# Two transformer blocks on one core: the tile scheduler orders the instructions by its timeline simulation

## The chip, the cores and the metric

The kernel runs on one core of one Trainium2 chip. The metric is the device time of one execution in microseconds (us), from a set of runs of which the median is given. Lower is better.

## The reference

The input is one sequence of 256 rows of width 2048. It goes through two blocks of different kinds, all in fp32. Cut to what matters here:

```python
# block 1
mod = silu(c) @ ada_w + ada_b            # (2048) @ (2048, 6*2048): shift, scale, gate, twice
h = rmsnorm(x, norm_mix_g) * (1 + scale_m) + shift_m
p = h @ w_in                             # 2048 x 11344: q, k, v, g, gate rank, latents, two merge gates
y_gla = gla(p) @ gla_wo                  # gated linear attention, 4 heads
y_mla = mla(p) @ mla_wo                  # latent attention, 16 heads, causal, with rope
x = x + gate_m * ((sigmoid(p_ga) * y_gla + sigmoid(p_gb) * y_mla) @ w_out)
h = rmsnorm(x, norm_ffn_g) * (1 + scale_f) + shift_f
x = rmsnorm(x + gate_f * swiglu(h, ffn_w_in, ffn_w_down), final_norm_g)
# block 2, for l in (0, 1)
h = rms_norm(x, pre_norm_g[l])
mixed = concat(retention(h), diff_attention(h), rg_lru(h))
x = x + rms_norm(mixed @ w_out[l], post_norm_g[l])
```

## The kernel before, in words

**The stream of weights.** Each weight matrix is read once, in blocks of 512 KB or 384 KB. `wload` (L172 to L175) gives the load to SP's queue into a tile `raw` (four buffers). `split` (L168 to L170) makes two halves of it for the matmuls: ACT casts the high half (`wh`, L169), DVE subtracts it to get the low half (`wl`, L170); there are six buffers of each. The activations are held split in the same way, as `hh` and `hl` (or `oh` and `ol` for what comes out of an attention).

**The products.** `lin` (L228 to L258) takes the blocks in groups of four and issues, for each 128 rows of weight and each of the two row tiles, three matmuls into one tile `pm` of PSUM (four buffers):

```python
pe.matmul(o, AH[:, k0 + k, sl], L[:, k, 0:nw], ...)   # L247: needs wl and hh
pe.matmul(o, AH[:, k0 + k, sl], H[:, k, 0:nw], ...)   # L248: needs wh and hh
pe.matmul(o, AL[:, k0 + k, sl], H[:, k, 0:nw], ...)   # L249: needs wh and hl
```

**The start stage.** The first projection runs in four groups of 512 rows of the 2048 (the loop over `KG`, from L577 on). In each group the product goes through three column parts: the latents (`latb`), then the two merge gates (`X` and `ga`), then a piece of v. L598 copies the first group's sums out, L600 on DVE adds those of the later groups. A group can start when its part of `mod` is known: the sum `acc` of `ada_w` over its rows (L351, L353 on DVE, from `raw` tiles of its own), four transposes on PE (L314, `tp<-ident,acc`), four row sums on ACT (L316, `adac`), an addition on DVE (L317, `mod<-adac,vc`). Then ACT makes the group's activations (L590, four of them, `ht`), ACT casts them (L169, `hh`) and DVE subtracts (L170, `hl`). The first group's scale does the sum with matmuls on PE instead (L349, `px`); the rows of x are normed and transposed for all groups at the start (L569, L570). The steps of the next group's `ada_w` sum are called between the column parts of the running group.

**The table of angles.** `later()` (L407 to L492) loads gains and positions with small DMAs and works out sines and cosines on DVE (`ext`, `latb`, L439 to L491) and ACT (L488, L492). The program calls it in the last group, after its second column part (`LATER = (3, 1)`).

**The GLA heads.** For each head `gla_att` folds six levels of a decay matrix: DVE and ACT make `gqk`, PE multiplies it with itself (L871, `px<-gqk`), DVE masks the result (L877, `ms`). Between these stand the matmuls of the projection of another part.

**The layer boundary of block 2.** At the end of the first layer DVE adds the normed product to X (L1359, `X<-y,r_y,X`), PE transposes X (L261), ACT and DVE split it into the next layer's `hh` and `hl` (L269, L270).

**What sets the order.** The kernel is written with the tile framework: the program issues instructions in the order of the Python code, and when the context closes, a scheduler puts them into one order for each engine, with the dependencies between them and a priority that counts up as the code is run. An engine runs its own list strictly in that order. The kernel steers the scheduler at a few places: `tc.high_priority(HP)` (L971, L1349) and `tc.issue_after(...)` (L976, L989, L1356) with the constants `PIN` and `PIN2`, the early or late call of generators (`AHEAD`, `LATER`, `PREP`), and the number of buffers. The context is opened in `kernel`.

## Time and profile before

| | before |
|---|---|
| median of 3 runs | 2666.24 us |
| lowest and highest of them | 2661.85, 2666.38 us |
| the profiled execution: its time, its span | 2668.47 us, 2666.7 us |
| mean granted clock of TensorE | 0.992 |
| busy: PE, DVE, ACT | 2590.0, 1829.1, 1332.0 us |
| read from memory | 555.77 MB |

The span runs from the first to the last instruction of the profiled execution, and its time lies 1.8 us above it. PE is TensorE's matmuls, PEld its weight loads, DVE VectorE, ACT ScalarE, SP the engine that issues the DMAs. A matmul with 512 columns is listed with 0.39 us, and one starts every 0.23 us, since they overlap.

### The profile page before, as it was taken

To read this page: it belongs to the slowest core of one execution; us is meant where nothing else is said; L and a number is where in the kernel's file an instruction comes from. 1 tells how busy PE (TensorE), PEld (TensorE's weight loads), DVE (VectorE), ACT (ScalarE), POOL (GpSimd) and SP (SyncE) were. 2 spreads that over 40 slices of the span, in tenths; PEclk is the share of its full clock that TensorE was granted. 3 is DMA by queue.
4 is the path that set the end of the run, shared out by engine and by line. 5 is a ranking of instruction groups with operands and counts; after the bars stand their busy time and mean duration, and the time that the engine had idled before them with its cause. 6 is when DMAs were issued, how large, how long until landed. Compare 5 with 4: busy or idle time off the path is not lost.

```text
span 2666.7 us, 35520 instructions
## 1 busy us (share of the span) xinstructions
PE 2590.0 (97%) x12980; PEld 2196.0 (82%) x12980; DVE 1829.1 (69%) x3043; ACT 1332.0 (50%) x2068; POOL 0.2 (0%) x4
## 2 busy tenths in 40 slices
PE   7999999999999998999999999999999999999998
PEld 4888888877888776777888888889988988997897
DVE  5899877778777777667554555467676657676755
ACT  4545754345555334443344434455565546465653
POOL 0000000000000000000000000000000000000000
PEclk9999999999999999999999999999999999999999
DMA  9898746586576887788655555565455565655464
GB/s 325 317 308 248 221 135 218 186 268 218 179 237 210 283 281 248 237 267 273 203 190 189 189 190 189 190 195 181 149 170 171 185 201 167 189 171 153 160 205 146
DMA packets 319672, 562.84 MB, mean 211 GB/s; under 512 B 23812, under 2 KB 100488, under 8 KB 319240
## 3 DMA queue, kind: packets, MB, share of 16 engines
q1 hardware_dynamic: 319496, 560.56, 65.2%
q8 instruction: 102, 1.67, 0.3%
q14 instruction: 74, 0.61, 0.1%
HBM read 555.77 MB, written 4.72 MB: 210 GB/s over the span
## 4 chain that ended last, share of the span: by engine, by line
PE 69%; DMA 14%; DVE 9%; ACT 5%; issue 2%; SPq 0%; ACTq 0%; DVEq 0%
PE pm L247 19%; PE pm L248 19%; PE pm L249 19%; DMA raw<-in_ada_w_dram 6%; DVE wl L170 4%; ACT wh L169 3%; DMA raw<-in_w_in_dram 3%; DVE acc L353 2%; DMA raw<-in_w_out_dram 2%; DMA raw<-in_ffn_w_in_dram 2%; DMA raw<-in_gla_wo_dram 1%; DMA raw<-in_mla_wo_dram 1%; PE px L871 1%; PE tp L261 1%; PE pm L637 1%
## 5 line engine op out<-in xcount | busy, mean ns | idle before, releaser
L170 DVE TENSOR_TENSOR wl<-raw,wh 128x1024 fp32r<-128x1024 f32 (+2 forms) x876 | 1005.1, 1155 | 469.7 <-ACT wh L169 444.5
L169 ACT CAST wh<-raw 128x1024 fp32r<-128x1024 f32 (+2 forms) x876 | 871.2, 998 | 817.0 <-PE pm L249 415.7
L247 PE MATMUL pm<-wl,hh 128*128 128x512 f32 (+2 forms) x2448 | 925.6, 378 | 21.7 <-DVE wl L170 15.4
L248 PE MATMUL pm<-wh,hh 128*128 128x512 f32 (+2 forms) x2448 | 913.5, 373 | 0.0
L249 PE MATMUL pm<-wh,hl 128*128 128x512 f32 (+2 forms) x2448 | 912.8, 373 | 0.0
L247 PEld LDWEIGHTS pm<-wl,hh 128*128 128x128 f32 x2448 | 462.1, 189 | 98.3 <-DVE wl L170 27.7
L248 PEld LDWEIGHTS pm<-wh,hh 128*128 128x128 f32 x2448 | 462.6, 189 | 62.9 <-issue 2.7
L249 PEld LDWEIGHTS pm<-wh,hl 128*128 128x128 f32 x2448 | 461.7, 189 | 63.9
L247 PE MATMUL pm<-wl,oh 128*128 128x512 f32 x864 | 342.4, 396 | 3.8 <-DVE wl L170 3.6
L249 PE MATMUL pm<-wh,ol 128*128 128x512 f32 x864 | 337.9, 391 | 0.0
L248 PE MATMUL pm<-wh,oh 128*128 128x512 f32 x864 | 337.6, 391 | 0.0
L353 DVE SCALAR_TENSOR_TENSOR acc<-raw,cT,acc 128x512 f32<-128x512 f32 x345 | 258.0, 748 | 71.4 <-DMA raw<-in_ada_w_dram 66.1
L247 PEld LDWEIGHTS pm<-wl,oh 128*128 128x128 f32 x864 | 162.6, 188 | 40.9 <-DVE wl L170 7.6
L249 PEld LDWEIGHTS pm<-wh,ol 128*128 128x128 f32 x864 | 162.6, 188 | 34.3
L248 PEld LDWEIGHTS pm<-wh,oh 128*128 128x128 f32 x864 | 162.8, 188 | 33.0 <-issue 0.5
L213 PE MATMUL pm<-hh,wl 128*128 128x256 f32 x256 | 74.3, 290 | 3.5 <-DVE wl L170 3.5
L214 PE MATMUL pm<-hh,wh 128*128 128x256 f32 x256 | 73.1, 286 | 0.0
L215 PE MATMUL pm<-hl,wh 128*128 128x256 f32 x256 | 72.9, 285 | 0.0
L213 PEld LDWEIGHTS pm<-hh,wl 128*128 128x128 f32 x256 | 49.7, 194 | 5.3 <-DVE wl L170 3.9
L214 PEld LDWEIGHTS pm<-hh,wh 128*128 128x128 f32 x256 | 49.7, 194 | 0.9 <-issue 0.9
L170 DVE TENSOR_TENSOR ol<-tp,oh 128x512 fp32r<-128x512 f32 (+1 forms) x38 | 23.7, 629 | 38.5 <-ACT oh L169 38.5
L215 PEld LDWEIGHTS pm<-hl,wh 128*128 128x128 f32 x256 | 49.6, 194 | 0.0
(396 smaller groups left out, 2087.0 us busy)
## 6 DMA issues: line engine op xcount, KB each, us to landing
raw<-in_w_in_dram SPq DMA_DIRECT2D x224, 512.0 KB
raw<-in_ada_w_dram SPq DMA_DIRECT2D x192, 512.0 KB
raw<-in_ffn_w_in_dram SPq DMA_DIRECT2D x176, 512.0 KB
raw<-in_w_in_dram SPq DMA_DIRECT2D x192, 384.0 KB
raw<-in_w_out_dram SPq DMA_DIRECT2D x96, 512.0 KB
raw<-in_ffn_w_down_dram SPq DMA_DIRECT2D x88, 512.0 KB
raw<-in_mla_wo_dram SPq DMA_DIRECT2D x32, 512.0 KB
raw<-in_gla_wo_dram SPq DMA_DIRECT2D x32, 512.0 KB
```

What stands on the lines that cost most here:

```text
L169: act.copy(H, src)
L170: vec.tensor_sub(L, src, H.bitcast(F32))
L213: pe.matmul(o, L[:, k, c], AH[:, k0 + k], start=k0 + k == 0, stop=False)
L214: pe.matmul(o, H[:, k, c], AH[:, k0 + k], start=False, stop=False)
L215: pe.matmul(o, H[:, k, c], AL[:, k0 + k], start=False, stop=k0 + k == KA - 1)
L247: pe.matmul(o, AH[:, k0 + k, sl], L[:, k, 0:nw], start=first, stop=False)
L248: pe.matmul(o, AH[:, k0 + k, sl], H[:, k, 0:nw], start=False, stop=False)
L249: pe.matmul(o, AL[:, k0 + k, sl], H[:, k, 0:nw], start=False, stop=last)
L261: pe.transpose(ps[:, q], src[:, q * P:(q + 1) * P], ident)
L353: vec.scalar_tensor_tensor(acc[:, 0:w], r[:, k], col, acc[:, 0:w], ALU.mult, ALU.add)
L637: pe.matmul(ps, L, A[0][:, k], start=k == 0, stop=False)
L871: pe.matmul(o[:, t], qk[:, f, sl], rhs, start=f == 0, stop=f == 1)
```

## The change

One argument is added where the context is opened. The scheduler then chooses the next instruction by a simulation of the engines' timelines instead of by its plain ready times. The code that issues instructions isn't touched.

```diff
@@ -1394,7 +1394,7 @@
         aps[n] = nc.dram_tensor(f"in_{n}_dram", a.shape, mybir.dt.from_np(a.dtype), kind="ExternalInput").ap()
     out = nc.dram_tensor("out_0_dram", (1, S, D), F32, kind="ExternalOutput").ap()
-    with tile.TileContext(nc) as tc:
+    with tile.TileContext(nc, schedule_with_timeline_sim=True) as tc:
         tile_two_blocks(tc, aps, out)
     r = _run(nc, [arrays], core_ids=[0])
     return r.results[0]["out_0_dram"]
```

The set of instructions is the same before and after (12526 matmuls and transposes on PE, 3045 instructions on DVE, 1210 on SP). Their order differs on every engine: on average an instruction stands 11 places from where it stood on PE and on DVE, 5 on ACT and 3 on SP. Three places follow.

**The first loads, on SP.** Before, behind the loads of x:

```order
L174 DMA raw<-in_ada_w_dram 128x2x512 x2
L575 DMA X<-in_x_dram 128x2048 x2
L174 DMA raw<-in_ada_w_dram 128x2x512 x15
L174 DMA raw<-in_w_in_dram 128x2x368 x2
L174 DMA raw<-in_ada_w_dram 128x2x512
```

and now:

```order
L174 DMA raw<-in_ada_w_dram 128x2x512 x2
L575 DMA X<-in_x_dram 128x2048 x2
L174 DMA raw<-in_ada_w_dram 128x2x512 x5
L412 DMA latb<-in_norm_ffn_g_dram 16x128
L414 DMA latb<-in_pre_norm_g_dram 16x128 x2
L174 DMA raw<-in_ada_w_dram 128x2x512 x2
L415 DMA latb<-in_mla_q_norm_g_dram 4x128
L416 DMA latb<-in_mla_kv_norm_g_dram 4x128
L417 DMA latb<-in_diff_subln_g_dram 2x128
L418 DMA latb<-in_gla_onorm_g_dram 4x128
L419 DMA latb<-in_diff_subln_g_dram 2x128
L435 DMA pos_i<-in_positions_dram 128x2x1
```

The small loads of `later()` (thirteen with those that follow) have come from far behind to between the first loads of `ada_w`; three of the `ada_w` loads that stand there now are those of the second group.

**The start of the third group, on PE and DVE.** `tp_1380`, `adac_1381` and `ht_1472` are the third group's transposes, row sums and activations; `pm_1479` is its first product, `pm_1433` the last of the second group; `acc_1519` is already the sum for the fourth group. PE before, at the transposes:

```order
L247 MATMUL pm_1337<-wl_1347,hh_114 128x512
L248 MATMUL pm_1337<-wh_1346,hh_114 128x512
L249 MATMUL pm_1337<-wh_1346,hl_115 128x512
L314 MATMUL tp_1380<-ident_79,acc_1147 128x128 x4
L247 MATMUL pm_1392<-wl_1397,hh_114 128x512
L248 MATMUL pm_1392<-wh_1396,hh_114 128x512
```

and now:

```order
L247 MATMUL pm_1433<-wl_1443,hh_114 128x512
L248 MATMUL pm_1433<-wh_1442,hh_114 128x512
L249 MATMUL pm_1433<-wh_1442,hl_115 128x512
L314 MATMUL tp_1380<-ident_79,acc_1147 128x128 x4
L247 MATMUL pm_1433<-wl_1443,hh_114 128x512
L248 MATMUL pm_1433<-wh_1442,hh_114 128x512
L249 MATMUL pm_1433<-wh_1442,hl_115 128x512
L247 MATMUL pm_1479<-wl_1484,hh_114 128x368
L248 MATMUL pm_1479<-wh_1483,hh_114 128x368
```

Before, 48 matmuls stood between the transposes and the third group's first product; now three do. DVE before, from the end of the second group on:

```order
L170 TENSOR_TENSOR wl_1443<-raw_1440,wh_1442 128x1024
L317 TENSOR_TENSOR mod_100<-adac_1381,vc_95 128x4
L170 TENSOR_TENSOR wl_1484<-raw_1481,wh_1483 128x736
L600 TENSOR_TENSOR ga_124<-pm_1392,ga_124 128x512
L351 TENSOR_SCALAR acc_1519<-raw_1520,cT_98 128x512
L353 SCALAR_TENSOR_TENSOR acc_1519<-raw_1520,cT_98,acc_1519 128x512
L353 SCALAR_TENSOR_TENSOR acc_1519<-raw_1524,cT_98,acc_1519 128x512
L600 TENSOR_TENSOR ga_124<-pm_1393,ga_124 128x512
L170 TENSOR_TENSOR hl_115<-ht_1472,hh_114 128x1024
```

and now, from the addition of the second group's last product on:

```order
L600 TENSOR_TENSOR latb_117<-pm_1433,latb_117 128x512
L353 SCALAR_TENSOR_TENSOR acc_1519<-raw_1568,cT_98,acc_1519 128x512
L463 SCALAR_TENSOR_TENSOR ext_116<-ext_116 128x256
L170 TENSOR_TENSOR wl_1587<-raw_1584,wh_1586 128x736
L317 TENSOR_TENSOR mod_100<-adac_1381,vc_95 128x4
L353 SCALAR_TENSOR_TENSOR acc_1519<-raw_1572,cT_98,acc_1519 128x512
L463 SCALAR_TENSOR_TENSOR ext_116<-ext_116 128x256
L353 SCALAR_TENSOR_TENSOR acc_1519<-raw_1572,cT_98,acc_1519 128x512
L463 SCALAR_TENSOR_TENSOR ext_116<-ext_116 128x256
L353 SCALAR_TENSOR_TENSOR acc_1519<-raw_1616,cT_98,acc_1519 128x512
L485 TENSOR_TENSOR ext_116<-ext_116,latb_117 128x256
L353 SCALAR_TENSOR_TENSOR acc_1519<-raw_1616,cT_98,acc_1519 128x512
```

The addition to `mod` has come behind the last sums of the second group, and the angles (`ext`, `latb`), which stood in the fourth group, now stand among the second's and third's work. The subtraction `hl_115<-ht_1472` follows two rows further down.

**The folds of a GLA head, on PE.** `gqk_5043`, `gqk_5057` and `gqk_5072` are three levels in turn; `pm_5162` is the projection beside them. Before:

```order
L871 MATMUL px_5041<-gqk_5043 128x64 x4
L247 MATMUL pm_5162<-wl_5167,oh_2795 128x512
L248 MATMUL pm_5162<-wh_5166,oh_2795 128x512
L249 MATMUL pm_5162<-wh_5166,ol_2796 128x512
L871 MATMUL px_5041<-gqk_5057 128x64 x4
L247 MATMUL pm_5162<-wl_5167,oh_2795 128x512
L871 MATMUL px_5070<-gqk_5072 128x64 x4
L248 MATMUL pm_5162<-wh_5166,oh_2795 128x512
```

and now, at the second of the three levels:

```order
L248 MATMUL pm_5162<-wh_5178,oh_2795 128x512
L249 MATMUL pm_5162<-wh_5178,ol_2796 128x512
L247 MATMUL pm_5162<-wl_5185,oh_2795 128x512
L248 MATMUL pm_5162<-wh_5184,oh_2795 128x512
L249 MATMUL pm_5162<-wh_5184,ol_2796 128x512
L247 MATMUL pm_5162<-wl_5185,oh_2795 128x512
L248 MATMUL pm_5162<-wh_5184,oh_2795 128x512
L249 MATMUL pm_5162<-wh_5184,ol_2796 128x512
L871 MATMUL px_5041<-gqk_5057 128x64 x4
L871 MATMUL px_5070<-gqk_5072 128x64 x4
L247 MATMUL pm_5163<-wl_5167,oh_2795 128x512
L248 MATMUL pm_5163<-wh_5166,oh_2795 128x512
```

Between the levels of `gqk_5043` and `gqk_5057` there now stand 24 matmuls of the projection instead of three; the third level still follows close behind the second.

## Rows read from the trace of the kernel before

**Rows 1.** The page: busy time of each engine, and its share of the span

```profile
PE 2590.0 (97%) x12980; PEld 2196.0 (82%) x12980; DVE 1829.1 (69%) x3043; ACT 1332.0 (50%) x2068; POOL 0.2 (0%) x4
```

**Rows 2.** Windows: us, then PE, PEld, DVE, ACT, POOL busy; clock; DMA share; GB/s

```profile
100.00:150.00 50.00, 49.25 (x238) 42.48 (x237) 47.32 (x66) 24.96 (x40) 0.00 (x0) 1.00 0.95 346
150.00:200.00 50.00, 47.62 (x231) 41.15 (x232) 46.59 (x63) 23.57 (x35) 0.00 (x0) 0.99 0.90 293
200.00:250.00 50.00, 50.00 (x234) 42.86 (x233) 45.98 (x73) 24.34 (x41) 0.00 (x0) 0.97 0.83 258
250.00:300.00 50.00, 49.75 (x232) 40.57 (x231) 48.34 (x129) 39.25 (x63) 0.00 (x0) 1.00 0.76 230
500.00:550.00 50.00, 44.36 (x212) 37.21 (x211) 35.03 (x74) 15.57 (x26) 0.00 (x0) 0.90 0.57 184
550.00:600.00 50.00, 45.51 (x277) 39.86 (x276) 38.26 (x55) 27.38 (x45) 0.00 (x0) 0.97 0.81 267
700.00:750.00 50.00, 48.14 (x236) 39.38 (x234) 36.33 (x82) 24.34 (x42) 0.00 (x0) 0.93 0.58 185
850.00:1075.00 225.00, 204.46 (x883) 160.19 (x881) 171.03 (x223) 94.66 (x131) 0.00 (x0) 0.98 0.82 271
1275.00:1900.00 625.00, 625.00 (x2915) 530.63 (x2914) 353.33 (x451) 278.96 (x339) 0.00 (x0) 1.00 0.59 190
2200.00:2250.00 50.00, 48.19 (x235) 40.01 (x233) 34.73 (x84) 29.61 (x66) 0.00 (x0) 1.00 0.55 163
```

**Rows 3.** Waits of PE: us in total, times, longest

```profile
PE pm L247 <- DVE wl L170: 19.0, 20, 4.6
...
PE px L871 <- DVE ms L877: 7.8, 3, 5.4
PE tp L261 <- DVE mg L958: 5.6, 4, 2.3
```

**Rows 4.** Chain, 0 to 60 us: start, us, what

```profile
0.73 0.39 SPq L105
...
25.25 4.12 DMA raw<-in_ada_w_dram
29.41 1.89 PE px L349 x4
31.32 3.90 DMA raw<-in_ada_w_dram
...
40.14 2.08 ACT xg L590 x4
...
42.91 0.96 ACT hh L169
```

**Rows 5.** Lines of DVE by form, 50 to 300 us: busy, mean ns, idle before

```profile
L353 DVE SCALAR_TENSOR_TENSOR acc<-raw,cT,acc 128x512 f32<-128x512 f32 x83 | 61.8, 746 | 1.0
L170 DVE TENSOR_TENSOR wl<-raw,wh 128x736 fp32r<-128x736 f32 x20 | 18.0, 918 | 2.5 <-ACT wh L169 2.4
...
L463 DVE SCALAR_TENSOR_TENSOR ext<-ext 128x256 f32<-128x256 f32 x9 | 3.7, 413 | 0.0
...
L600 DVE TENSOR_TENSOR latb<-pm,latb 128x512 f32<-128x512 f32 x4 | 2.7, 682 | 0.0
...
L461 DVE TENSOR_SCALAR ext<-ext 128x256 f32<-128x256 f32 x4 | 1.1, 283 | 0.0
L317 DVE TENSOR_TENSOR mod<-adac,vc 128x4 f32<-128x4 f32 x6 | 1.0, 160 | 2.7 <-ACT junk L316 2.6
...
L439 DVE CAST pos_f<-pos_i 128x4 f32<-128x4 int32 x1 | 0.2, 161 | 0.0
```

**Rows 6.** Timeline of PE at the third group's transposes: start, us, instruction

```profile
160.90 0.60 PE L314 MATMUL tp<-ident,acc 128*128 128x128 f32 x4
```

**Rows 7.** Timeline of PE at the GLA folds

```profile
515.51 1.76 PE L871 MATMUL px<-gqk 128*128 128x64 f32 x7 [5.39 <-DVE ms L877]
```

**Rows 8.** Timeline of DVE at the layer boundary of block 2

```profile
2229.16 2.08 DVE L1359 SCALAR_TENSOR_TENSOR X<-y,r_y,X 128x512 f32<-128x512 f32 x3
```

## The prediction

> **What bounds the kernel now.** I read the page first, then the stretches, the waits of PE, and last the timelines of the places where the order changes. On the page the reader is to see that PE is busy for 2590.0 us of the 2666.7 us span, and that DVE (1829.1 us) and ACT (1332.0 us) are far below it [rows 1]. The set of instructions doesn't change, so a better order can win at most the 77 us in which PE stands idle, and what a lower clock costs. A worse order has no such limit.
>
> The stretches say where these 77 us are. Look at the first number behind the length, PE's busy time, and at the clock, third from the end. From 1275 to 1900 us PE is busy for all of 625.00 us: no order can gain there. Between 850 and 1075 us it is idle for 225 - 204.46 = 20.5 us while the DMA engines are busy for 0.82 of the time. From 500 to 550 us it is idle for 5.6 us at a clock of 0.90, from 550 to 600 us for 4.5 us at 0.97, from 700 to 750 us for 1.9 us at 0.93 [rows 2]. The clock has two levels, 1.2 and 2.4 GHz, so 0.90 of full speed over 50 us means that 10 us passed at the lower one, which costs 5 us of work; 0.97 costs 1.5 us and 0.93 3.5 us. With that the three stretches lose 10.6, 6.0 and 5.4 us.
>
> One more thing in the stretches: from 100 to 300 us DVE is busy for 47.3, 46.6, 46.0 and 48.3 of each 50 us [rows 2]. In the start stage there are two engines at their limit, and what is put on DVE's list ahead of something that PE needs can't hide.
>
> **The change part by part.** Most moves are by a few places among equals and cost nothing: PE has four PSUM tiles and six split blocks ahead of it, and the stretch without any idle time shows that this covers small shifts. I price the places where a move is longer than this cover.
>
> *First loads: +4 us.* The chain of the start is made of loads of `ada_w` and PE's sums over them: 4.12 us for one load, 1.89 us for its matmuls, 3.90 us for the next load; then come the activations, and the cast before the first product ends at 43.9 us [rows 4]. Now three more loads of this kind, for the second group, and thirteen small DMAs stand among them on SP's queue. Issuing a small one takes 0.39 us [rows 4], so thirteen take 5 us if nothing hides them; they hide where SP would have waited for a buffer anyway, and a load that waits costs 3.9 to 4.1 us once. Bounds 0 and 9 us; I take one load time, 4 us, since SP does wait for buffers in this stretch.
>
> *Second group: +2 us.* DVE's list has some 9 us more ahead of this group's `hl`, parts of the angles and of the next sum. Only L249 needs `hl`, and PE's list now has eight matmuls of L247 and L248 to run ahead; a matmul starts every 0.23 us, so they cover 1.8 us. Bounds 0 (DVE runs ahead) and 7 us (9 less the cover); I take 2 us, nearer to the lower end, because the casts for `hh` stand as before.
>
> *Third group: +14 us.* Before, PE ran the transposes of the sum at 160.90 us [rows 6], with 48 matmuls behind them, that is 11 us of cover for the way over ACT and DVE to `hh`. Now three matmuls are left, 0.7 us. The way itself: four row sums on ACT, the addition to `mod` (0.16 us [rows 5]), then four L590 in 2.08 us and the cast in 0.96 us [rows 4]. On DVE the addition stands behind work that must be done first. Between the last L353 of this sum and the addition there are seventeen instructions: four L600 at 0.68 us, three L353 at 0.75 us, four `wl` at 0.92 us, and six pieces of the angles at 0.28 to 0.42 us, 10.8 us in all [rows 5]. If DVE is on time, only the last four of them come after PE's last product (0.68 + 0.75 + 0.41 + 0.92 = 2.8 us), and PE stands for 2.8 + 0.2 + 2.1 + 1.0 - 0.7 = 5.4 us. If DVE is late, all seventeen count: 10.8 + 3.2 - 0.7 = 13.3 us. The angles make it late. They are 44 instructions with 14.6 us (22 groups of this view, the first and last in [rows 5]), and they have come from the fourth group to a stretch in which DVE was idle for only 2.7 and 3.4 us of each 50 [rows 2]. So I take 11 us, near the upper end. A stall also lowers the clock: the stretch with the 5.39 us wait [rows 7] has 0.90 [rows 2], which I counted as 5 us. I add 3 us, between that and nothing, since not every wait shows it (the start stage has 0.97 to 1.00 now).
>
> The Trainium skill (TensorE: Matmul & The Clock Gate, "What's actually happening") says that the array's clock is halved when PE has been idle and comes back only when it has been busy again. By that rule the 3 us are sure to be paid; by the rows alone they lie between 0 and 5 us.
>
> *Fourth group: -3 us.* The angles are gone from DVE's list from 235 us on, where DVE was the fullest (48.34 of 50 us) and the clock fell to 0.97 in the 50 us before [rows 2]. What PE lost there is 2 us in the 150 to 200 stretch, 1.5 us by the clock and 0.3 us of idle time; of these 4 us I take 3. Bounds -4 and 0.
>
> *GLA folds: -12 us.* At 510 us PE has three matmuls between one level and the next and then waits for 5.39 us for DVE's mask [rows 7]. Now 24 stand there, 5.5 us, which is the length of the wait. The wait should go and the clock stay up: of the 10.6 us lost in this stretch I take 7.5, as the third level still follows close on the second. From 550 to 600 us ACT's casts come ahead of the row sums and table loads that they stood behind; of 6.0 us I take 3. From 700 to 750 us the folds are spread in the same way; of 5.4 us I take 1.5. All together 12 us; bounds 3 us (only the waits' halves) and 20 us.
>
> *850 to 1275 us: -2 us.* PE waits there for loads and splits; the longest item of PE's waits is `wl` with 19.0 us in the whole span, and the transposes of `mg` cost 5.6 us [rows 3]. The order of the loads hardly changes, so the first stays. The transposes stand 2 to 15 matmuls later: of 5.6 us I take 2. Bounds -5 and +3 us, the latter because a later transposition also starts the next product later.
>
> *Layer boundary of block 2: +4 us.* Before, DVE mixes the splits of the next layer's `hl` with the additions to X, which take 0.7 us each [rows 8]. Now the splits of the second half come behind six `wl` and the whole norm of the last column. Followed along the list, this `hl` is up to 8 us later than L249 needs it. PE lost 1.8 us in this stretch so far [rows 2]. Bounds -1.8 and +8; I take the middle, 4 us.
>
> **The sum.** 4 + 2 + 14 - 3 - 12 - 2 + 4 = +7 us. Against the profiled execution's 2668.47 us that is 2675.5 us. The median of the runs, 2666.24 us, lies 2.2 us lower, so I predict 2673 us, 0.26% more than the median. A measurement of this kernel tells a difference from none at about 0.2%, which is 5.3 us.
>
> **The rivals.**
>
> *DVE's lead covers the third group (faster).* If DVE enters the group boundary on time, the stall is 5.4 us instead of 11, with no drop of the clock. What decides is whether DVE has the 14.6 us of the angles done by then in gaps: its idle time between 100 and 200 us is 6.1 us [rows 2], and PE's delay of 4 to 6 us from the first loads and the second group gives it as much again. That is about 11 us, not 14.6, so it falls a little short. In this case the start costs 4 + 0 + 5 - 3 = +6 us, and with the GLA folds at -17 us, the loads at -4 and the boundary at 0 the sum is -15 us: 2651 us by the median. For it: the folds' gain stands on a measured wait, the losses on how far DVE is behind.
>
> *Both sides cancel (no change).* PE is busy for 97% of the span, and each stretch is limited by the same engine as before. With the start at +12 us, the folds at -11 and the rest at 0, the time is about 2667 us. For it: the two large terms are of one size. It needs nothing new, only each to be off by a few us.
>
> *The folds don't gain (much slower).* DVE makes the levels of `gqk` and masks them on the same list, and the projection's `wl` stand between. If 24 matmuls on PE bring 24 matmuls' worth of splits onto DVE ahead of the mask, the mask is as late as before. The waits for `ms` are three with 7.8 us in all [rows 3], so this mechanism takes back 8 to 10 of the 12 us, and with the boundary at +8 us the sum is +20 us: 2686 us. Against it: on DVE the order there puts the parts of the folds ahead of some of the splits.
>
> **How the numbers follow.** The forecast (2664 to 2680 by its own bounds, the most of it above 2671) and the much slower case together get 0.46 for slower by over 0.2%: 0.33 and 0.13. No change gets 0.27, the faster case 0.27. The range is to hold 8 in 10: 2652 at the low end, the faster case's time, and 2690 at the high end, some us above the much slower one.
>
> **What would show it.** In the changed profile the stretch from 150 to 200 us should have some 10 us of idle PE time, in one wait for `hh` (or `ht`), with a clock below 0.95 behind it; the first product should start at about 48 us. The waits for `ms` should be gone or below 2 us, and the stretch that was 500 to 550 us at a clock near 1.00. A new wait for `hl` should stand near 2235 us. I am wrong if the product of the third group starts without a wait of more than 5 us, if the folds' wait only moves to another level, or if a long wait appears between 1275 and 1900 us, where I price nothing.

## The result, and the profile after

| | before | after |
|---|---|---|
| median of the runs | 2666.31 us (4 runs) | 2704.19 us (4 runs) |
| lowest and highest | 2661.85, 2670.56 us | 2702.07, 2706.53 us |
| span of the profiled execution | 2666.7 us | 2702.5 us |

The change makes the kernel slower by the factor 1.0136, with a 95% interval from 1.012 to 1.0153: some 36 us, where 7 us were forecast. The span grew by 35.8 us.

The page's first part for the kernel after, busy time of each engine:

```profile
PE 2596.4 (96%) x12980; PEld 2211.2 (82%) x12980; DVE 1825.9 (68%) x3043; ACT 1329.4 (49%) x2068; POOL 0.2 (0%) x4
```

PE's busy time is 6.4 us above that of [rows 1] for the same instructions; the mean clock is 0.985 instead of 0.992, which goes the same way, though no run here splits the 6.4 us. The other 29 us of the 35.8 are new idle time of PE. Nothing more is read or computed.

The stretches of the kernel after, with the columns of [rows 2]:

```profile
100.00:150.00 50.00, 50.00 (x244) 43.48 (x243) 48.25 (x79) 27.48 (x48) 0.00 (x0) 1.00 0.91 307
150.00:200.00 50.00, 44.13 (x205) 38.82 (x205) 48.37 (x82) 20.93 (x36) 0.00 (x0) 0.93 0.84 273
200.00:250.00 50.00, 50.00 (x226) 41.32 (x225) 43.50 (x63) 23.75 (x37) 0.00 (x0) 1.00 0.76 238
...
500.00:550.00 50.00, 49.79 (x267) 42.30 (x266) 42.37 (x83) 20.13 (x31) 0.00 (x0) 1.00 0.73 239
550.00:600.00 50.00, 45.61 (x251) 38.72 (x249) 39.88 (x66) 24.12 (x44) 0.00 (x0) 0.97 0.84 268
700.00:750.00 50.00, 49.83 (x266) 42.24 (x265) 38.50 (x81) 26.27 (x41) 0.00 (x0) 1.00 0.61 187
1050.00:1100.00 50.00, 43.79 (x193) 34.71 (x192) 28.64 (x52) 27.43 (x57) 0.00 (x0) 0.93 0.52 178
1275.00:1900.00 625.00, 624.98 (x2892) 527.96 (x2891) 356.27 (x451) 279.92 (x338) 0.00 (x0) 1.00 0.60 191
2100.00:2150.00 50.00, 44.86 (x228) 39.58 (x227) 28.18 (x67) 24.78 (x56) 0.00 (x0) 0.93 0.38 113
2250.00:2300.00 50.00, 42.91 (x209) 37.21 (x208) 38.07 (x114) 31.31 (x71) 0.00 (x0) 0.86 0.46 137
2550.00:2600.00 50.00, 44.86 (x247) 41.38 (x247) 32.83 (x79) 27.33 (x61) 0.00 (x0) 0.93 0.46 139
```

Read it against [rows 2]. From 500 to 550 us and from 700 to 750 us PE has become busy and its clock is 1.00: the folds of the GLA heads no longer stop it. From 150 to 200 us it is idle for 5.9 us (2.4 before) at a clock of 0.93 (0.99 before). And there are four holes at 1050, 2100, 2250 and 2550 us, where the old kernel has none or a shallower one:

```profile
1050.00:1100.00 50.00, 47.55 (x220) 37.77 (x219) 33.09 (x57) 31.10 (x59) 0.00 (x0) 1.00 0.59 200
2100.00:2150.00 50.00, 50.00 (x275) 47.18 (x275) 28.04 (x38) 25.05 (x37) 0.00 (x0) 1.00 0.61 195
2250.00:2300.00 50.00, 50.00 (x290) 49.14 (x289) 33.69 (x86) 26.94 (x41) 0.00 (x0) 1.00 0.62 184
2550.00:2600.00 50.00, 50.00 (x252) 44.55 (x252) 27.27 (x30) 24.50 (x32) 0.00 (x0) 1.00 0.64 210
```

Windows of equal times compare different work once one kernel runs late. So I also followed the instructions. Both kernels issue the same set, and at some points of time all instructions that the old kernel had started are also exactly those that stand first in the new lists. At such a point **lateness** is the start of PE's last instruction in a run less its start in the profile of the old kernel (for instance, the first product starts at 43.9 us in the old profile and at 50.6 us in the new: 6.7 us late). Its growth between two points is what the stretch between them costs.

```
us in the old trace    320   770   850  1035  1105  1275  1900  2160  2225  2270  2655
lateness, new order   14.1   0.8   0.8   1.6   8.6  17.5  17.2  21.9  21.9  32.6  35.8
```

The start costs 14.1 us, latent attention and GLA win 13.3 back, and at 770 us the new kernel is level. It then loses 16.7 us in the 850 to 1275 us that are fed by loads (7.0 of them in the entry of the feed-forward part, 1035 to 1105), 4.7 and 3.1 us in the mixers of the two layers of block 2, and 10.7 us at the boundary between the layers. With 0.3 us won from 1275 to 1900 us the sum is 35.8 us.

The waits of PE in the kernel after, whole span, that answer to [rows 3]:

```profile
PE pm L247 <- DVE wl L170: 31.3, 19, 4.5
...
PE pm L247 <- ACT hh L169: 12.4, 3, 6.2
PE tp L1309 <- DVE de L1305: 7.2, 2, 3.6
...
PE tp L261 <- ACT tT L278: 3.8, 4, 1.2
PE pm L247 <- ACT hh L269: 3.4, 5, 0.9
...
PE tp L261 <- DVE mg L958: 1.5, 3, 0.9
```

The wait for `ms` is gone from the list and that for `mg` fell from 5.6 to 1.5 us, as forecast. The wait for `wl` grew from 19.0 to 31.3 us. Among the new waits are those of the difference attention's transposes for `de`, 3.6 us in each layer, and those of the feed-forward entry for `tT`.

### The profile page after: what moved, and what is told of

Same layout as the page of the kernel before. It is cut to its first block, busy times and chain, and to the rows that moved or that the text cites. A ratio compares the mean times of both kernels' runs of the same rounds, so it can differ in the third digit from the quotient of the medians.

```text
span 2702.5 us, 35513 instructions
## 1 busy us (share of the span) xinstructions
PE 2596.4 (96%) x12980; PEld 2211.2 (82%) x12980; DVE 1825.9 (68%) x3043; ACT 1329.4 (49%) x2068; POOL 0.2 (0%) x4
## 4 chain that ended last, share of the span: by engine, by line
PE 76%; DMA 12%; DVE 7%; ACT 2%; issue 2%; SPq 0%; DVEq 0%; ACTq 0%
PE pm L247 22%; PE pm L248 21%; PE pm L249 21%; DMA raw<-in_ada_w_dram 7%; DVE wl L170 3%; DMA raw<-in_ffn_w_in_dram 2%; DVE acc L353 2%; ACT wh L169 1%; PE tp L261 1%; DMA raw<-in_gla_wo_dram 1%; DMA raw<-in_w_in_dram 1%; PE pm L637 1%; DMA raw<-in_w_out_dram 1%; PE pm L639 1%; PE pm L638 1%
## 5 line engine op out<-in xcount | busy, mean ns | idle before, releaser
L353 DVE SCALAR_TENSOR_TENSOR acc<-raw,cT,acc 128x512 f32<-128x512 f32 x345 | 257.5, 747 | 113.7 <-DMA raw<-in_ada_w_dram 111.0
L170 DVE TENSOR_TENSOR ol<-tp,oh 128x512 fp32r<-128x512 f32 (+1 forms) x38 | 23.7, 629 | 31.3 <-ACT oh L169 31.3
```

The lines of the kernel that those rows point to most:

```text
L170: vec.tensor_sub(L, src, H.bitcast(F32))
L353: vec.scalar_tensor_tensor(acc[:, 0:w], r[:, k], col, acc[:, 0:w], ALU.mult, ALU.add)
```

## The experiments

All experiments use one tool. `pin_order`, called behind the program, reads a table of instruction numbers and ties each instruction of an engine to the one before it in the table, so that the scheduler has no choice left. With the table of one kernel it issues that kernel's order. A mixed table takes some stretches, cut at the points above, from the old order and the others from the new. Every such run is the kernel before with its table; the code is cut to what matters here.

```diff
+def pin_order(tc, nc):
+    for names in table:                       # one list for each of PE, DVE, ACT, SP
+        ins = {i.name: i for i in nc.cur_bb.bb.instructions}
+        for a, b in zip(names, names[1:]):
+            tc.add_manual_dep(ins[b], a, mybir.DependencyInfo(mybir.DependencyClass.NoSync, mybir.DependencyReason.DATA), reason="pin_order")
     with tile.TileContext(nc) as tc:
         tile_two_blocks(tc, aps, out)
+        pin_order(tc, nc)
```

Below, a diff names only what the table takes. Each run was timed beside the old kernel on the same chip; "above the old" is the ratio to it times 2667 us. The new kernel itself stands at 36 us.

No run ties one whole order as a control. But where a table holds the old order in parts that aren't fed by loads, lateness stands still: in the run with the GLA part alone (below) it is -16.2 us at 1275 us and -16.1 us at 2655 us. So the tying itself shows no cost.

Lateness comes from one profile of each run, and a stretch with one and the same order differs from run to run. In the runs that left the new order on all lists of a stretch, the start cost 12.8 to 15.4 us (13 runs), the entry of the feed-forward part 5.7 to 9.2 us (12 runs), the load-fed part behind it 6.1 to 14.0 us (11 runs), the boundary 8.3 to 10.7 us (13 runs), the mixers 3.3 to 4.8 and 3.1 to 4.7 us (15 runs). Latent attention and GLA won 10.2 to 15.5 us in all 19 runs that have the new order there. What a run gives back has to be read against these spreads.

### Where the time goes: one stretch put back

**The feed-forward stretch.**

```diff
-table: new order
+table: new order; 1035 to 1275 us: old order of PE, DVE, ACT, SP
```

> The new order everywhere, except that the instructions which ran from 1035 to 1275 us in the trace of the old order (end of w_out, the entry of the feed-forward part and the stretch fed by loads) are pinned to their old order on all four engines. Local theory: the stretch lost 17 us by its own order, since the work done at 1035 us was 0.2 us late and that at 1275 us 17.2 us late; expected 2704 - 17 = 2687 us (2684 to 2690). Rival: this stretch is limited by loads, and the loss comes from what it inherits (buffers, the state of the queue); then the old order gives back less than half, and the time stays above 2695 us.

Measured: 2690.97 us, ratio 1.0096 [1.0078, 1.0114], 26 us above the old instead of 36. Lateness grew from 2.5 to 5.9 us over the stretch, against 1.6 to 17.5 us with the new order. The time is 1 us above the range that the local theory asked for, and the theory holds for the most part; the 3.4 us that stay lie in the spread that the old order itself shows there (below).

**The layer boundary.**

```diff
-table: new order
+table: new order; 2225 to 2270 us: old order of PE, DVE, ACT, SP
```

> The new order everywhere, except that the instructions of 2225 to 2270 us of the old trace (layer boundary of block 2) are pinned to their old order. Local theory: -10.8 us, 2693.5 us (2691 to 2696). Rival (the boundary loses because ACT and DVE come into it late from before): less than 4 us given back, above 2700 us.

Measured: 2694.85 us, ratio 1.0103 [1.0088, 1.0118]. Lateness is 21.7 us on both sides of the stretch: the boundary costs nothing in the old order, and 10.7 us in the new. By the ratios of the times the run gives back some 9 us.

**The start.**

```diff
-table: new order
+table: new order; 0 to 320 us: old order of PE, DVE, ACT, SP
```

> The new order everywhere, except that everything of the first 320 us of the old trace is pinned to its old order. Local theory: the start costs 13.9 us, expected 2690 us (2687 to 2693). Rival (later stretches gain because the start runs ahead, so that a faster start is given back in the stages fed by loads): above 2697 us.

Measured: 2687.92 us, ratio 1.0071 [1.0056, 1.0086], 19 us above the old. The start's cost is given back in full, and later stretches keep their gains and losses: the GLA part wins 14.7 us here too (lateness -2.2 to -16.9).

**The mixers of block 2.**

```diff
-table: new order
+table: new order; 1900 to 2160 and 2325 to 2580 us: old order of PE, DVE, ACT, SP
```

> The new order everywhere, except that the instructions of 1900 to 2160 us and of 2325 to 2580 us of the old trace (the three mixers of each layer of block 2) are pinned to their old order. Local theory: the two stretches cost 4.9 and 3.1 us, since the last two heads of the difference attention come back to back with nothing beside them; expected 2704 - 8 = 2696 us (2693 to 2699). Rival (these waits only take the place of work that was done earlier there): less than 3 us given back, above 2701 us.

Measured: 2695.29 us, ratio 1.0114 [1.0086, 1.0143]. Lateness stays at 17.0 us over the first stretch and at 25.4 over the second, so the 4.7 and 3.1 us are theirs. The times alone wouldn't show it, since this ratio's interval overlaps that of the new kernel. The timeline of PE in the kernel after shows what happens there:

```profile
2125.54 0.92 PE L1288 MATMUL px<-dqkT 64*128 64x128 f32 x4
2127.18 0.92 PE L1288 MATMUL px<-dqkT 64*128 64x128 f32 x4 [0.72 <-DVE y L1319]
2131.70 0.45 PE L1309 MATMUL tp<-ident,de 128*128 128x128 f32 x1 [3.61 <-DVE de L1305]
```

The scores of the last two heads (L1288) and the transposes of the last softmax (L1309) follow one another with no product between them. The whole softmax lies open, 3.61 us. The products which stood between them in the old order have been issued earlier; 41 matmuls of products stand in a row just ahead of this place. By this timeline the new order spent its cover before the chain that needed it; no run moved these products alone.

**The change in the GLA part alone.**

```diff
-table: old order
+table: old order; 320 to 770 us: new order of PE, DVE, ACT, SP
```

> The old order everywhere, except that the instructions of 320 to 770 us of the old trace (latent attention and the GLA heads) are in the new order: the change made in this part alone. Local theory: lateness falls there from 13.9 to 0.8 us, so this kernel is 13 us faster than the old one, 2653 us (2650 to 2656). Rival (the gain was only the start's delay made up, work that was late anyway): within 4 us of the old kernel, 2662 to 2668 us.

Measured: 2653.3 us, ratio 0.9953 [0.9935, 0.9971], 12.5 us faster than the old kernel. Lateness falls from -1.6 to -15.3 us in the part and is -16.1 us at the end. So the gain was real and not time made up, and this kernel beats both.

### What in the stretches costs it: single lists put back

**The entry of the feed-forward part.** In the old order the four transposes of each row tile (L261) lie among the products; in the new one they stand in a row. On ACT, two casts of blocks stand ahead of the scaling L278 of the last two. Two runs put one side back each.

```diff
-table: new order
+table: new order; 1035 to 1105 us: old order of ACT and DVE
```

> The new order everywhere, except that ACT's and DVE's lists alone are pinned to the old order from 1035 to 1105 us of the old trace (entry of the feed-forward part, which lost 8.2 us); PE and SP keep the new one. Theory A (ACT's casts of blocks that have not landed stand ahead of the scaling L278 that is ready, so that hh is late): at least 6 us given back, 2698 us or less. Theory B (PE's own list is the cause: four transposes in a row and the first product behind all of them): less than 3 us given back, 2701 us or more.

```diff
-table: new order
+table: new order; 1035 to 1105 us: old order of PE
```

> The counterpart of the run in which ACT and DVE alone went back and the time rose by 4 us: now PE's list alone is pinned to the old order from 1035 to 1105 us of the old trace, ACT, DVE and SP keep the new one. Theory B (PE's list, with four transposes in a row and the first product behind them, is the cause): at least 6 of 8.2 us given back, 2698 us or less. Theory C (the lists fit one another, and any one put back alone spoils the rest): no gain, 2703 us or more.

Measured: 2707.85 us, ratio 1.0154 [1.0131, 1.0177], and 2706.1 us, ratio 1.0143 [1.0124, 1.0162]. Over these 70 us lateness grew by 6.0 and 9.3 us; with all lists new by 7.0 (5.7 to 9.2 over the runs), with all four old (in the run with the whole stretch put back) by -0.3. Both theories that named one side fell. Theory C is what is left, that PE's early transposes, ACT's scaling and DVE's splits fit one another. It isn't shown: the three lists together were not put back, and SP's list has twelve loads in other places here (the reloads of x and of the gate's bias, `xr` and `gf`, among the weights), which no run put back alone.

**The layer boundary.** The same question there:

```diff
-table: new order
+table: new order; 2225 to 2270 us: old order of ACT and DVE
```

> The new order everywhere, except that ACT's and DVE's lists alone are pinned to the old order from 2225 to 2270 us of the old trace (layer boundary); PE and SP keep the new one. Theory A (the splits L269 and L270 stand behind wl, the norm and the row sums L161): at least 7 of the 10.8 us given back, 2697 us or less. Theory B (PE's transposes stand too early in its list, ahead of products that would cover the way over ACT and DVE): less than 4 us, 2700 us or more.

```diff
-table: new order
+table: new order; 2225 to 2270 us: old order of PE
```

> The counterpart at the layer boundary, where ACT and DVE alone gave back 3.7 of some 10 us: PE's list alone is pinned to the old order from 2225 to 2270 us of the old trace. Theory B (PE's list is the larger part): 5 to 8 us given back, 2696 to 2699 us. Theory C (the lists only work together): less than 2 us given back, 2702 us or more.

Measured: 2700.48 us, ratio 1.0125 [1.0101, 1.0149], and 2706.74 us, ratio 1.0145 [1.0129, 1.0162]. The boundary cost 4.7 us with ACT's and DVE's lists old, 9.8 us with PE's alone old. Against the 8.3 to 10.7 us of the runs with the new order, ACT's and DVE's lists give back some 4 to 6 us, less than the 7 us that theory A asked for, and PE's list alone gives nothing that stands out. What carries the rest stays open: the lists together, or SP's list, which has twelve loads in other places here too. The ratios' intervals of both runs overlap that of the new kernel, so this rests on lateness alone. Here the windows of the kernel after show the price of a hole:

```profile
2245.00:2255.00 10.00, 9.99 (x49) 8.14 (x47) 7.96 (x18) 5.00 (x8) 0.00 (x0) 1.00 0.40 117
2255.00:2265.00 10.00, 5.05 (x13) 3.00 (x14) 9.49 (x30) 8.40 (x26) 0.00 (x0) 0.64 0.54 174
2265.00:2275.00 10.00, 8.32 (x39) 7.00 (x37) 5.42 (x30) 4.76 (x13) 0.00 (x0) 0.84 0.14 32
```

PE is busy for half of the second row while DVE is busy for 9.49 of 10 us: the splits of `hl`, the norm and `wl` all want DVE there. The clock falls to 0.64 and is still at 0.84 ten us later. The longest single wait of PE around this place is only 1.9 us, so a list of waits by length would hide this place.

**The load-fed part, 1105 to 1275 us.** SP's list is the same in both orders there. On DVE the new order puts sums L353 of `ada_w` blocks ahead of splits `wl` of blocks that are already cast. The waits of DVE in this part, first in the old kernel:

```profile
DVE wl L170 <- ACT wh L169: 25.9, 26, 2.2
DVE acc L353 <- DMA raw<-in_ada_w_dram: 17.8, 12, 3.5
```

and in the kernel after:

```profile
DVE acc L353 <- DMA raw<-in_ada_w_dram: 25.6, 16, 3.7
DVE wl L170 <- ACT wh L169: 24.1, 25, 1.9
```

DVE waits 7.8 us more for `ada_w`, and PE's waits for `wl` in the part grow from 4.0 to 11.0 us. That looked like the cause:

```diff
-table: new order
+table: new order; 1105 to 1275 us: old order of DVE
```

> The new order everywhere, except that DVE's list alone is pinned to the old order from 1105 to 1275 us of the old trace (the rest of the feed-forward stretch that is fed by loads, which lost 8.8 us); PE, ACT and SP keep the new one, and SP's is the same in both. Theory (DVE's list has the sums L353 of ada_w blocks, whose loads come last, ahead of the splits wl of blocks that are there, so that DVE waits for a load with ready work behind it): at least 6 us given back, 2698 us or less. Rival (PE's list, which now takes turns between the two row tiles): less than 3 us given back, 2701 us or more.

Measured: 2702.78 us, ratio 1.0132 [1.0113, 1.0151]. The part cost 7.6 us instead of 8.9, inside the spread of the new order. The theory fell as the single cause. PE's list, and both together:

```diff
-table: new order
+table: new order; 1105 to 1275 us: old order of PE
```

> The new order everywhere, except that PE's list alone is pinned to the old order from 1105 to 1275 us of the old trace; read by how much later the work at 1275 us is than in the old trace, against that at 1105 us (8.9 us with all lists new). Theory (PE's turns between the row tiles are the cause): below 4 us. Rival (DVE waits for late blocks of ada_w ahead of ready splits, and PE's list only passes it on): 7 us or more.

```diff
-table: new order
+table: new order; 1105 to 1275 us: old order of PE and DVE
```

> The same stretch with PE's and DVE's lists both pinned to the old order, ACT and SP new. Theory C (only both lists together bring it back): lateness grows by 2 to 4 us over the stretch, as in the run that had all four lists old there (3.7 us), while each list alone leaves 7 us or more. Rival (ACT's casts are the cause): 7 us or more here too.

Measured: 2707.25 us, ratio 1.0152 [1.013, 1.0174], and 2703.26 us, ratio 1.0134 [1.0113, 1.0154]. The part cost 10.7 and 8.3 us, both inside the spread of the new order: neither brings it back. The last two runs put all four lists back, in the part alone and in the entry alone:

```diff
-table: new order
+table: new order; 1105 to 1275 us: old order of PE, DVE, ACT, SP
```

> The new order everywhere, except that all four lists are pinned to the old order from 1105 to 1275 us of the old trace; the entry of the feed-forward part stays new. Read by lateness at 1275 us less that at 1105 us. Theory (the order of this part is the cause, ACT's list with the others): 2 to 4 us, as with entry and part both old (3.7). Rival (the entry's new order hands the loss on): 7 us or more.

```diff
-table: new order
+table: new order; 1035 to 1105 us: old order of PE, DVE, ACT, SP
```

> The new order everywhere, except that all four lists are pinned to the old order from 1035 to 1105 us of the old trace, the entry of the feed-forward part; the load-fed part behind it stays new. Theory (each part costs by its own order): the entry costs about 0 instead of 7 us, the part behind it still 7 us or more. Rival (the loss is handed on): 2 to 4 us in the part behind it.

Measured: 2698.88 us, ratio 1.0097 [1.0074, 1.0119], and 2695.45 us, ratio 1.0087 [1.0069, 1.0106]. With the entry new and the part old, the part cost 4.9 us, between what the two theories asked for. With the entry old and the part new, the entry cost 0.6 us and the part 6.1. So the entry's loss is its own and isn't handed on. For the load-fed part only ranges can be given: in all runs with the new order there it cost 6.1 to 14.0 us, in the five runs with the old order on all four lists 1.8 to 4.9 us (4.9 here, 3.7 in the run with the whole feed-forward stretch old, and 1.8, 3.8 and 2.8 in the three mixes on the old order). They don't overlap: the order costs some 6 us, the difference of the two means (9.5 and 3.4 us). The old order's runs all lie above 0, so the profile of the old kernel that lateness is read against is a fast one in this part, and some 3 of the 8.9 us are not the order's. By which instruction the order costs its 6 us stays open; ACT's list, with 8 instructions in other places, was not tried alone.

### How the start divides

**Angles late.** Here the scheduler itself made the start's order, with its timeline simulation on and the work and the loads of `later()` held back (`hl_ins` is the fourth group's `hl`, `ld_ins[0]` the last load before it). This edit made the table; the run ties that order for the first 320 us:

```diff
-                    later()
+                    with tc.issue_after(hl_ins.ins), tc.issue_after(ld_ins[0].ins):
+                        later()
-table: new order
+table: new order; 0 to 320 us: the order that this gives
```

> The new order everywhere, except in the first 320 us, where the scheduler (with its timeline simulation) was told to put what later() does on DVE behind the fourth group's hl, and its small loads behind the fourth group's loads. Theory A (the angles on a full DVE and the small loads make the start's 13.9 us): the first product comes within 2 us of the old trace's 43.9 us, the wait ahead of the third group is below 2 us, time 2692 us or less. Theory B (the transposes of the third group's sum stand too late in PE's list whatever DVE does, and the second group's loads and the order of PE's sums delay the start): the wait ahead of the third group stays above 4 us, the first product comes after 47 us, time 2698 us or more.

Measured: 2696.29 us, ratio 1.0114 [1.009, 1.0139]. Stretches of this kernel:

```profile
150.00:200.00 50.00, 50.00 (x244) 43.46 (x243) 48.64 (x68) 25.02 (x41) 0.00 (x0) 1.00 0.93 315
200.00:250.00 50.00, 50.00 (x241) 43.21 (x241) 43.02 (x68) 23.31 (x34) 0.00 (x0) 1.00 0.68 215
250.00:300.00 50.00, 49.42 (x220) 40.56 (x218) 44.00 (x108) 36.50 (x52) 0.00 (x0) 1.00 0.70 220
300.00:350.00 50.00, 44.22 (x311) 39.47 (x311) 35.38 (x91) 29.09 (x75) 0.00 (x0) 0.93 0.54 170
```

The wait ahead of the third group is gone: PE is busy for all of 100 us, better than in the old kernel. The first product comes at 48.3 us (43.9 in the old, 50.6 in the new, and up to 52.8 in the runs with the new start). So 4.4 us of the 6.7 us that the first product is late stay with the angles and the small loads held back, and 2.2 us or a little more went with them. The loss has moved: from 300 to 350 us PE is idle for 5.8 us, 4.7 of them ahead of a transposition (L529) behind DVE's splits of the normed latents (`cql`, L270) and 1.4 us in waits for the transposed table of angles (`trT`). Lateness at 320 us is 6.4 us instead of 14.1. Theory A holds for the third group; the first product (4.4 us late where 2 were allowed) and the total (2692 us or less) stay short of what it asked for.

**The first loads alone.**

```diff
-table: new order
+table: new order; 0 to 45 us: old order of PE, DVE, ACT, SP
```

> The new order everywhere, except that the instructions of the first 45 us of the old trace are pinned to their old order (first loads, PE's first sums and transposes of x, the first split). Theory: the first product starts within 1 us of the old 43.9 us (new: 50.6), the wait ahead of the third group stays at 6 us, and lateness at 320 us falls from 14.1 to 7.5 us; time 2697.5 us. Rival (DVE, not the loads, limits the first 300 us): the first product is early, but lateness at 320 us stays above 11 us.

Measured: 2709.59 us, ratio 1.0158 [1.0135, 1.0181], slower than the new kernel. This run failed as an experiment, and its timeline of DVE says why:

```profile
44.89 1.22 DVE L170 TENSOR_TENSOR hl<-xg,hh 128x1024 fp32r<-128x1024 f32 x1
54.43 0.17 DVE L439 CAST pos_f<-pos_i 128x4 f32<-128x4 int32 x1 [8.32 <-DMA pos_i<-in_positions_dram]
```

and of PE:

```profile
55.48 0.68 PE L247 MATMUL pm<-wl,hh 128*128 128x368 f32 x1 [9.06 <-DVE wl L170]
```

The first product came at 44.8 us as expected, and lateness at 320 us was 18.3 us. But the mix kept the angles early on DVE and moved the load of the positions behind the first weights: SP issued it at 51.7 us, where the new kernel does at 20.6 us. So DVE stood for 8.32 us ahead of splits that were ready, and PE for 9.06 us behind it. The run therefore decides nothing between its two theories, and how the 4.4 us that stay of the late first product divide is open.

### A version that beats both

```diff
-table: old order
+table: old order; 320 to 770, 850 to 870 and 1020 to 1035 us: new order of PE, DVE, ACT, SP
```

> The old order everywhere, except that 320 to 770, 850 to 870 and 1020 to 1035 us of the old trace are in the new order: all the stretches between two points where both orders have issued the same instructions, in which the new order lost no time. Theory (gains of such stretches add up): 14.5 us as in the run with 320 to 770 us alone, and 1.8 + 3.3 us more, so 18 to 20 us faster than the old order, 2647 to 2650 us. Rival (in the stretches fed by loads the small gains are given back until the next load): 2652 to 2654 us, as without them.

Measured: 2657.11 us, ratio 0.9959 [0.9943, 0.9975]: the small pieces in the load-fed part added nothing, as the rival said; the time even lies above the rival's 2654 us.

```diff
-table: old order
+table: old order; 320 to 770 us: new order; 45 to 238 us: the order with the angles late
```

> The old order, with the new one from 320 to 770 us (12.5 to 14.5 us faster so far) and, from 45 to 238 us, the order which the timeline simulation gives when the angles are held back behind the fourth group. In the run with the angles late PE was idle for no part of 150 to 250 us, where the old order has 2.4 us and 1.5 us of clock. Theory (these gains add up): 2650 us, 16 to 17 us faster than the old order. Rival (DVE is at its limit there, and what is won up to 238 us is lost again before 320): 2653 us, as without.

Measured: 2651.81 us, ratio 0.994 [0.992, 0.9961], 16 us faster than the old kernel. PE has no idle time at all from 50 to 350 us in it; these are two of its rows:

```profile
150.00:200.00 50.00, 50.00 (x245) 43.40 (x244) 48.69 (x68) 24.43 (x41) 0.00 (x0) 1.00 0.94 317
200.00:250.00 50.00, 50.00 (x242) 43.20 (x241) 43.73 (x71) 25.58 (x40) 0.00 (x0) 1.00 0.66 210
```

Its lateness at 320 us is -4.2 us, 2.6 us better than in the run with the GLA part alone (-1.6), but at the end both stand at -16 us, and their intervals overlap. So it beats the old kernel, and that it beats the GLA part alone isn't shown.

## Why the prediction was wrong

The sign was right and the size was not: 7 us forecast, 36 us measured, outside the range. Two steps failed: the stretch fed by loads was priced at -2 us, and the mixers of block 2 at nothing. A third, the layer boundary, was right in kind and too small. By its steps:

- **First loads, +4 us.** The first product starts at 50.56 us: +6.7 us. Within the bounds. The forecast took one load time for the small loads and the second group's loads together; 4.4 us stay when the small loads and the angles are held back.
- **Second, third and fourth group, +2, +14 and -3 us.** The wait came where it was forecast, ahead of the third group's first product. Two rows of DVE, and behind them that of PE, whose last product before it ends at 177.4 us:

```profile
177.46 0.69 DVE L600 TENSOR_TENSOR latb<-pm,latb 128x512 f32<-128x512 f32 x1
...
179.90 0.15 DVE L317 TENSOR_TENSOR mod<-adac,vc 128x4 f32<-128x4 f32 x1
```

```profile
183.29 0.67 PE L247 MATMUL pm<-wl,hh 128*128 128x368 f32 x1 [5.87 <-ACT hh L169]
```

  I had worked out 5.4 us for the case that DVE is on time and 13.3 us for DVE late, and took 11. DVE was on time: it adds the second group's last product as soon as PE has made it, and the addition to `mod` follows 2.4 us later. The lower end was right, and the argument that the angles make DVE late was wrong. The clock in that stretch is 0.93, which is 3.5 us, where I took 3 between 0 and 5: the granted clock is 0.50, the lower level, from 183 to 187 us, and 1.00 again from 191 us on. The rule that the Trainium skill gives (TensorE: Matmul & The Clock Gate, "What's actually happening"), that the clock is halved after PE has been idle and comes back once it is busy, agrees with this trace.

  By lateness the second group cost nothing (6.7 us at the first product, 5.1 us at 171 us), the third 8.7 us (13.8 us at 177 us), and 4.2 us were won back by 205 us, about what the fourth group's term had. Then 5.1 us were lost from 296 to 313 us, at the transposes of the latents, which had no price. So the start's total, 14.1 us against +17, is nearer than its parts, and that is luck.
- **GLA folds, -12 us.** 13.3 us by lateness, and 12.5 us by the time of the run with this part alone. The mechanism was right: the 5.39 us wait [rows 7] is gone and the clock stays at 1.00. The parts came out otherwise: 9.0 us won at the first folds (509 to 547 us, 7.5 forecast) and 5.3 us from 711 to 744 us (1.5 forecast), only 0.4 us from 560 to 606 us (3 forecast), and latent attention, which had no price, lost 4.1 us (322 to 503 us). That the total fits is in part luck too.
- **850 to 1275 us, -2 us.** This is the step that failed most. It measured +16.7 us, far outside its bounds of -5 and +3; in the seven other runs that left it as it was it cost 15.5 to 20.4 us. I wrote that "the order of the loads hardly changes, so the first stays", the first being PE's wait for `wl`. The loads' order did stay from 1105 to 1275 us, but in that part PE's wait for `wl` grew from 4.0 to 11.0 us, and in the entry ahead of it PE waits 3.8 us for `tT`, where it had no such wait. I priced the one wait that I could see shrink (`mg`, which did fall by 4.1 us) and no wait that could grow. That the order costs it is shown by the runs that put it back; by which instructions is open.
- **Layer boundary, +4 us.** 10.7 us (8.3 us at least in the other runs). The place was right, and the mechanism, splits that come late on ACT and DVE, carries some 4 to 6 us of it. The term was mis-sized: I took 4 us between -1.8 and +8 (the middle is 3.1) and no clock, which falls to 0.64 there.
- **"Most moves are by a few places among equals and cost nothing."** True from 1275 to 1900 us, where lateness changes by 0.3 us. Not true in the mixers of block 2, with 7.8 us: there instructions of the heads moved by more than 200 places on PE, which the comparison of the orders tells, and I gave it no price.
- **The rivals.** The third group's stall was as small as the faster case had it, but its clock fell, which that case had excluded, and the folds gained 13.3 us, not 17. The much slower case had the boundary near its size, but its folds did gain. The load-fed stretch and the mixers stand in no rival.
- **The signs of being wrong.** None of the three came: the third group's wait was over 5 us, the folds' wait was gone, and no long wait appeared between 1275 and 1900 us. They watched three places, and most of the error came from others.

Of the 29 us between forecast and measurement, 18.7 are the load-fed stretch, 7.8 the mixers and 6.7 the boundary; the start and the folds take back 4.2.

## What to carry to other kernels

A scheduler's order can be taken apart: find the points where both orders have issued the same instructions, read lateness there, and keep each stretch from the order that is better in it. Keep only gains that stand out of what the same order varies by: the small pieces of the load-fed part added nothing here. Price the stretches fed by loads and those between two layers first, and look for waits that can grow and for covers that have been issued too early, not only for waits that might go. And lists that a scheduler made together should be moved together: one engine's list put back gave 1.3 us at most in four runs here, which is inside the spread. Why the simulation prefers the orders that lost time, no run here shows.

## What the runs showed that I had not expected

A stretch's cost isn't a sum over its lists: in the feed-forward entry neither PE's list nor ACT's and DVE's together gave back more than 1.0 us, and all four gave 7.3. The load-fed part behind it spread by several us between runs, also where its own order was one and the same: 1.8 to 4.9 us with the old order, 6.1 to 14.0 us with the new. And a small load can be dear where it stands: the positions, 256 numbers in each of two loads, held DVE for 8.32 us in the mixed start, because they were issued behind the first weights.
